# Preparing the S5 constants on GpSimd instead of VectorE, with the preparation's start moved, in a two-layer streaming encoder

## The chip, the cores and the metric

The kernel runs on one core of a Trainium2 chip. The metric is the device time of one execution in microseconds (us); the median of several runs counts. TensorE is called PE here, VectorE DVE, ScalarE ACT, GpSimd POOL and SyncE SP, as in the profile.

## The reference, cut to what matters

A trunk of two layers works on 256 positions of width 1024 in float32. Each layer is an FFN, a mixer and a second FFN, each added to the residual stream with a norm before and after.

```python
def reference(x, ...):
    for l in range(DEPTH):                      # DEPTH = 2
        f1 = swiglu(rmsnorm(x, g[0]), gate[l, 0], up[l, 0], down[l, 0])
        x = x + 0.5 * rmsnorm(f1, g[1])
        m = hybrid_mixer(rmsnorm(x, g[2]), ...)
        x = x + rmsnorm(m, g[3])
        f2 = swiglu(rmsnorm(x, g[4]), gate[l, 1], up[l, 1], down[l, 1])
        x = x + 0.5 * rmsnorm(f2, g[5])
```

The mixer projects the stream once, runs an S5 state-space model and a chunked attention with a relative bias on parts of it, and merges the two through gates. The S5 part needs constants that depend on its parameters alone:

```python
dt = exp(log_dt); mag = exp(lr * dt); ang = li * dt
ab_re, ab_im = mag * cos(ang), mag * sin(ang)
den = lr * lr + li * li
f_re = ((ab_re - 1) * lr + ab_im * li) / den
f_im = (ab_im * lr - (ab_re - 1) * li) / den
bb = f * b                                      # complex
```

The kernel also needs cos and sin of `ang` times 1, 2, 4, ... 64, to build tables of rotations by a position within a chunk. All of it is computed on the chip, once for each layer.

## The kernel before

**Weights.** All weight matrices are read from HBM in 368 chunks of 128 x 1024 float32, 184 for each layer: 66 for the first FFN, 52 for the mixer, 66 for the second FFN. A chunk lands in a `raw` buffer (`load`, line 461), ACT rounds it to a high part `wh` and DVE subtracts that from the chunk to get the low part `wl` (`halves`, line 467). Each product is then three matmuls: high by high, high by low, low by high. For every third chunk from 44 to 65 of a layer (`ADDED`) the subtraction is a DMA instead: ACT writes `-wh` into `wl` and POOL starts a DMA that adds the chunk to it (`add_to`, line 380). SP issues all loads.

**Positions.** The 256 positions are two tiles of 128, t=0 and t=1. Chunk i is used for both, t=1 some chunks behind t=0.

**Blocks of an FFN.** The hidden width is cut into six blocks. A block has eight chunks for gate and up, and four down chunks of the block before it are worked in. In some blocks (`SEVEN`: 1 and 3 in the first FFN, 1 to 4 in the second) gate and up for both tiles are formed by seven products in place of eight (`seven`, line 649). They need sums and differences of eight chunks, which lie in eight `raw` buffers for that time; some of these sums are made by DVE, those of `BY_DMA` by DMA adds that POOL starts.

**Buffers.** `SLOTS` gives 33 `blk` (128 x 512), 12 `raw`, 8 `wh`, 8 `wl`, 8 PSUM banks `ps`, and a few small ones. Buffers of the classes in `ORDERED` are handed out in the order of due times.

**The order.** Nothing is issued as it is written. Every operation is recorded with an engine, a planned cost, its inputs and outputs and a stream; `schedule` (line 209) then works back from the consumers to a due time for every operation (with a margin, `MARGIN`, where one stream feeds another) and simulates the engines, giving each the ready operation that is due first. The result is one fixed order for each engine, and every engine works through its own in order, waiting where an input or a buffer isn't ready.

**The preparation.** `prep(l)` (line 797) is recorded once for each layer before its mixer, in the stream `prep` with a margin of 40 us. Nothing of it may start before the first matmul of chunk `PREP_AT[l]` for t=0, and the loads of the attention's bias not before that of chunk `BIAS_AT` of the layer:

```python
after = [self.g.ops[self.mark[(0, PREP_AT[l])]]]
...
early = [self.g.ops[self.mark[(0, l * LAYER_CHUNKS + BIAS_AT)]]]
```

Once that gate is open, `constants` (line 781) takes `raw` buffers for `mt` and for the two rotation tables `E` and lets POOL set their first columns. The parameters come by DMA into `prm`. Then some 80 short operations on DVE, through the helpers `tt` (line 376), `stt` (395) and `ts` (400), form `dt` and `mag` by a polynomial exponential on 16 columns, the angles on 16 and then 112 columns (7 multiples of 16), their sine and cosine, and the factors `fr` and `fi`. ACT spreads `mag2` into `mt`. Wider operations follow on DVE: the complex products `cmul` and the doubling steps for `E`; ACT and PE put `BT`, `CT` and `D0` together. The mixer's S5 part (`s5`) reads all of these.

**POOL's queue.** Besides the memsets of the preparation POOL starts the DMA adds and computes the reciprocal square root of every norm as a power (`pow`, line 391), all in one queue.

Of the kernel before, what the change touches and what calls it, by code (L numbers as in the profile page):

```python
# [17 lines left out]
ALU = mybir.AluOpType  # L18
AX = mybir.AxisListType

P = 128
# [18 lines left out]
LAG = 3  # L40
TAU = 1.395
MARGIN = {"pre": 10.0, "edge": 4.0, "conv": 7.558, "conv0": 3.423, "task": 7.748, "att0": 37.576, "s50": 37.749, "att1": 28.585, "sums": 3.0, "s51": 29.753, "prep": 40.0}
PREP_AT = (3, 149)
BIAS_AT = 50
LOOK = 0.027
CAP = 5.417
WARM = 16
# [18 lines left out]
class View:  # L66
# [50 lines left out]
    def ap(self):  # L117
        t = self.buf.tile
        for s in self.steps:
            t = s(t)  # L120
        return t
# [202 lines left out]
class Kern:  # L324
# [51 lines left out]
    def tt(self, out, a, b, op):  # L376
        return self.g.op("dve", 0.07 + a.free_size() / 960, [out], [a, b],
                         lambda: self.nc.vector.tensor_tensor(out=out.ap(), in0=a.ap(), in1=b.ap(), op=op))  # L378
# [16 lines left out]
    def stt(self, out, a, s, b, op0=ALU.mult, op1=ALU.add):  # L395
        cost = 0.07 + a.free_size() / 960 + 0.061 * isinstance(s, View)
        return self.g.op("dve", cost, [out], [a, s, b], lambda: self.nc.vector.scalar_tensor_tensor(  # L397
            out=out.ap(), in0=a.ap(), scalar=ap(s), in1=b.ap(), op0=op0, op1=op1))

    def ts(self, out, a, s1, s2=None, op0=ALU.mult, op1=ALU.add):  # L400
        def fn():
            if s2 is None:
                self.nc.vector.tensor_scalar(out=out.ap(), in0=a.ap(), scalar1=ap(s1), scalar2=None, op0=op0)
            else:
                self.nc.vector.tensor_scalar(out=out.ap(), in0=a.ap(), scalar1=ap(s1), scalar2=s2, op0=op0, op1=op1)  # L405
        cost = 0.07 + a.free_size() / 1920 + 0.061 * isinstance(s1, View)
        return self.g.op("dve", cost, [out], [a, s1], fn)
# [389 lines left out]
    def prep(self, l):  # L797
        self.mode("prep", "bulk")
        if l == 0:
            self.S = [self.own(f"st{i}", [P, PAIRS, 65], F32) for i in range(2)]  # L800
        after = [self.g.ops[self.mark[(0, PREP_AT[l])]]]
        self.constants(after)
# [5 lines left out]
        self.bias = [[self.blk() for _ in range(2)] for _ in range(2)]  # L808
        early = [self.g.ops[self.mark[(0, l * LAYER_CHUNKS + BIAS_AT)]]]
        for par in range(2):  # L810
            for u in range(2):
                b = self.bias[par][u].rearrange("p (h k) -> p h k", k=256)
# [1 line left out]
                self.memset("pool", b[0:64, :, 192:256], MASK)  # L814
        self.prm = prm
        lr, li = prm[:, SP_LR:SP_LR + 16], prm[:, SP_LI:SP_LI + 16]
        ts, tt, stt = self.ts, self.tt, self.stt

        def tmp(nmx):
            return self.own(f"pt_{nmx}", [P, 16], F32)  # L820

        def exp(o, xin):
            n, r, p = tmp("en"), tmp("er"), tmp("ep")
            ib = self.own("pt_ei", [P, 16], I32)
            ts(n, xin, math.log2(math.e), MAGIC)
            ts(n, n, MAGIC, op0=ALU.subtract)
            stt(r, n, -0.693359375, xin)
            stt(r, n, 2.12194440054690583e-4, r)
            ts(p, r, 1.0 / 5040)
            for k in (720, 120, 24, 6, 2, 1):  # L830
                stt(p, p, 1.0 / k, r, ALU.add, ALU.mult)
            ts(n, n, -127.0, 128.0, ALU.max, ALU.min)
            ts(n, n, 127.0, 8388608.0, ALU.add, ALU.mult)
            self.copy(ib, n)
            stt(o, p, 1.0, ib.bitcast(F32), ALU.add, ALU.mult)

        dt, ld, mag, mag2 = tmp("dt"), tmp("ld"), tmp("mag"), tmp("mag2")
        exp(dt, prm[:, SP_DT:SP_DT + 16])
        tt(ld, lr, dt, ALU.mult)
        exp(mag, ld)  # L840
        tt(mag2, mag, mag, ALU.mult)
        self.mag2 = mag2
        self.act(self.mt[:, :, 1:], mag2.spread(63), AF.Copy)

        wk = [self.blk() for _ in range(2)]
        ang, k, z, sn, cs, m, a = (wk[i // 4][:, (i % 4) * 112:(i % 4) * 112 + 112] for i in range(7))
        angv = ang.rearrange("p (e j) -> p e j", j=16)
        tt(angv[:, 0, :], li, dt, ALU.mult)
        for e in range(1, 7):
            ts(angv[:, e, :], angv[:, 0, :], float(2 ** e))  # L850
        ts(k, ang, 2.0 / math.pi, MAGIC)
# [4 lines left out]
        stt(ang, k, -c1, ang)  # L856
        stt(ang, k, -c2, ang)
        stt(ang, k, -c3, ang)
        tt(z, ang, ang, ALU.mult)
        ts(sn, z, 1.0 / 362880)  # L860
        for q in (-1.0 / 5040, 1.0 / 120, -1.0 / 6):
            stt(sn, sn, q, z, ALU.add, ALU.mult)
# [8 lines left out]
        stt(a, m, -1.0, m, ALU.mult, ALU.max)  # L871
        ts(k, a, -1.0, 1.0)
        ts(a, a, -1.0, 2.0)
        tt(m, m, a, ALU.mult)
        ecs = self.own("ecs", [P, 7, 16], F32)
        esn = self.own("esn", [P, 7, 16], F32)
        ef, sf = ecs.rearrange("p e j -> p (e j)"), esn.rearrange("p e j -> p (e j)")
        tt(ef, cs, k, ALU.mult)
        tt(a, sn, m, ALU.mult)
        tt(ef, ef, a, ALU.subtract)  # L880
        tt(sf, sn, k, ALU.mult)
        tt(a, cs, m, ALU.mult)
        tt(sf, sf, a, ALU.add)
        self.ecs, self.esn = ecs, esn

        ar, ni, nr, den, fr, fi, q = (tmp(s) for s in ("ar", "ni", "nr", "den", "fr", "fi", "q"))
        tt(ar, mag, ecs[:, 0, :], ALU.mult)
        ts(nr, ar, 1.0, op0=ALU.subtract)
        tt(ni, mag, esn[:, 0, :], ALU.mult)
        tt(den, lr, lr, ALU.mult)  # L890
        tt(q, li, li, ALU.mult)
        tt(den, den, q, ALU.add)
        self.recip(den, den)
        tt(fr, nr, lr, ALU.mult)
        tt(q, ni, li, ALU.mult)
        tt(fr, fr, q, ALU.add)
        tt(fr, fr, den, ALU.mult)
        tt(fi, ni, lr, ALU.mult)
        tt(q, nr, li, ALU.mult)
        tt(fi, fi, q, ALU.subtract)  # L900
        tt(fi, fi, den, ALU.mult)

        def half(t, i):
            return t[:, 256 * i:256 * i + 256].rearrange("p (j h) -> p j h", h=16)
# [51 lines left out]
        for e in range(6):  # L956
            k = 2 ** e
# [369 lines left out]
```

## Time and profile before

| | us |
|---|---|
| median of 3 runs | 1128.24 |
| lowest and highest | 1126.39, 1130.42 |
| the profiled execution | 1127.01 |
| its span | 1125.2 |

The span runs from the first to the last instruction in the profile; the mean granted clock of PE in it is 0.997 of full speed. The profile gives each engine's busy time, and for each instruction its start, its length and what the engine waited for before it. Operations that go through a helper carry the helper's line, so the names of the buffers tell them apart. PE's matmuls are pipelined, and one of 128 x 512 is shown longer than the distance to the next.

### The profile page before, as it was taken

The page shows a single profiled execution, that of the slowest core. Times are in us where ns is not written, and L with a number is a line of the kernel's source. Part 1 is how long each engine was busy: PE and PEld are TensorE (multiplying, and loading weights), DVE is VectorE, ACT ScalarE, POOL GpSimd, SP SyncE. Part 2 cuts the span into 40 slices and gives each one's busy share as a digit, 9 for nine tenths or more (in the row PEclk, how much of TensorE's full clock was granted, in tenths as well). Part 3 has the DMA queues.
Part 4 walks back from the last instruction along what each step waited for, and adds up shares of the span by engine and source line. Part 5 has one row for each costly group of instructions (what it writes and reads, how often), then busy time and mean ns, then how long its engine had stood idle before and what let it go on. Part 6 is the DMA issues. An engine that isn't in the chain of part 4 may idle for free.

```text
span 1125.2 us, 15956 instructions
## 1 busy us (share of the span) xinstructions
PE 1107.9 (98%) x5728; PEld 885.6 (79%) x5728; DVE 954.2 (85%) x1402; ACT 749.1 (67%) x1066; POOL 99.4 (9%) x131
## 2 busy tenths in 40 slices
PE   8999999999999999999999999999999999999997
PEld 6778788777788888788887888887777888888886
DVE  6998995895977899899899689778959679999983
ACT  6957686647754697577577476856486546878752
POOL 1101111000000031010030011100000002111100
PEclk9999999999999999999999999999999999999999
DMA  9885997545275557899658669964535664789941
GB/s 343 228 314 129 328 295 235 169 136 164 97 251 197 179 122 217 269 283 278 243 162 263 229 181 325 276 213 148 170 112 181 195 212 143 214 219 268 293 167 38
DMA packets 69487, 238.61 MB, mean 212 GB/s; under 512 B 8096, under 2 KB 8864, under 8 KB 69408
## 3 DMA queue, kind: packets, MB, share of 16 engines
q1 hardware_dynamic: 60192, 204.03, 51.2%
q0 software_dynamic: 9216, 33.56, 16.3%
q8 instruction: 45, 0.74, 0.3%
q14 instruction: 34, 0.28, 0.1%
HBM read 202.96 MB, written 1.05 MB: 181 GB/s over the span
## 4 chain that ended last, share of the span: by engine, by line
PE 87%; DVE 5%; issue 2%; ACT 2%; DMA 2%; POOL 1%; SPq 0%; POOLq 0%; DVEq 0%; ACTq 0%
PE ps L418 81%; PE ps L432 4%; DVE wl L378 3%; DMA raw<-in_wall_dram 2%; PE ps L424 1%; DVE blk L378 1%; ACT blk L371 1%; POOL s L393 1%; ACT wh L371 1%; DVE blk L397 1%; DVE raw L378 0%; SPq L354 0%; DVE x L397 0%; DVE s L405 0%; POOLq L1322 0%
## 5 line engine op out<-in xcount | busy, mean ns | idle before, releaser
L418 PE MATMUL ps<-wh,blk 128*128 128x512 f32 x2848 | 878.0, 400 | 4.5 <-DVE blk L378 2.3
L418 PEld LDWEIGHTS ps<-wh,blk 128*128 128x128 f32 x2848 | 530.4, 188 | 127.6 <-DVE blk L378 3.9
L371 ACT ACTIVATE wh<-raw 128x1024 fp32r<-128x1024 f32 (+1 forms) x442 | 456.9, 1053 | 261.0 <-PE ps L418 200.4
L378 DVE TENSOR_TENSOR wl<-raw,wh 128x1024 fp32r<-128x1024 f32 (+1 forms) x426 | 505.7, 1215 | 104.3 <-ACT wh L371 103.7
L418 PE MATMUL ps<-wl,blk 128*128 128x512 f32 x1424 | 524.4, 399 | 0.9 <-DVE wl L378 0.8
L418 PEld LDWEIGHTS ps<-wl,blk 128*128 128x128 f32 x1424 | 267.5, 188 | 63.4 <-DVE wl L378 2.5
L371 ACT ACTIVATE blk<-ps 128x512 fp32r<-128x512 f32 (+4 forms) x156 | 86.5, 561 | 54.8 <-PE ps L432 30.2
L378 DVE TENSOR_TENSOR blk<-ps,blk 128x512 fp32r<-128x512 f32 (+2 forms) x164 | 109.4, 672 | 13.1 <-ACT blk L371 12.7
L432 PE MATMUL ps<-ident,blk 128*128 128x128 f32 x432 | 74.7, 273 | 0.0
L382 POOL DMA_DIRECT2D raw<-raw x48 | 41.6, 867 | 341.3 <-ACT raw L371 261.8
L393 POOL TENSOR_TENSOR s<-s,mhalf 128x1 f32<-128x1 f32 x24 | 32.1, 1338 | 448.3 <-DVE s L405 448.2
L371 ACT ACTIVATE blk<-blk 32x128 f32<-32x128 f32 (+4 forms) x148 | 59.1, 400 | 12.4 <-DVE blk L378 8.6
L432 PEld LDWEIGHTS ps<-ident,blk 128*128 128x128 f32 x432 | 54.6, 140 | 15.9 <-PE ps L418 1.3
L371 ACT ACTIVATE blk<-ps,s 128x512 f32<-128x512 f32 (+1 forms) x68 | 43.7, 655 | 24.6 <-PE ps L418 20.4
L378 DVE TENSOR_TENSOR raw<-raw,raw 128x1024 f32<-128x1024 f32 x48 | 58.1, 1219 | 0.1
L371 ACT ACTIVATE raw<-raw 128x1024 f32<-128x1024 f32 x48 | 50.2, 1053 | 4.3 <-DVE raw L378 3.9
L378 DVE TENSOR_TENSOR blk<-blk,blk 128x512 f32<-128x512 f32 (+3 forms) x70 | 42.3, 627 | 0.0
L371 ACT ACTIVATE blk<-blk,s 128x128 f32<-128x128 f32 (+2 forms) x76 | 34.6, 486 | 6.7 <-DVE blk L378 6.6
L397 DVE SCALAR_TENSOR_TENSOR blk<-blk,s,blk 128x512 f32<-128x512 f32 x44 | 32.0, 746 | 0.9 <-ACT blk L371 0.8
L397 DVE SCALAR_TENSOR_TENSOR blk<-ps,s,blk 128x512 f32<-128x512 f32 (+1 forms) x24 | 15.8, 658 | 9.7 <-ACT blk L371 9.4
L382 POOL DMA_DIRECT2D wl<-raw x16 | 13.8, 865 | 111.7 <-ACT wl L371 56.3
L378 DVE TENSOR_TENSOR blk<-ps,raw 128x512 f32<-128x512 f32 x32 | 19.8, 681 | 4.2 <-PE ps L418 4.2
(100 smaller groups left out, 434.0 us busy)
## 6 DMA issues: line engine op xcount, KB each, us to landing
raw<-in_wall_dram SPq DMA_DIRECT2D x366, 512.0 KB, 5.3
raw<-raw POOLq DMA_DIRECT2D x48, 512.0 KB, 5.3
wl<-raw POOLq DMA_DIRECT2D x16, 512.0 KB, 7.2
gain<-in_gains_dram SPq DMA_DIRECT2D x22, 256.0 KB, 4.3
blk<-in_bias_dram SPq DMA_DIRECT2D x8, 256.0 KB, 4.8
raw<-in_wall_dram SPq DMA_DIRECT2D x4, 256.0 KB, 4.3
blk<-in_sp_dram SPq DMA_DIRECT2D x4, 256.0 KB, 9.3
x<-in_x_dram SPq DMA_DIRECT2D x3, 256.0 KB, 5.8
```

Source lines behind the costliest of these rows:

```text
L371: self.nc.scalar.activation(out=out.ap(), in_=in_.ap(), func=func, **k)
L378: lambda: self.nc.vector.tensor_tensor(out=out.ap(), in0=a.ap(), in1=b.ap(), op=op))
L382: lambda: self.nc.gpsimd.dma_start(out=out.ap(), in_=in_.ap(), accum_op=ALU.add), func="dma")
L393: lambda: self.nc.gpsimd.tensor_tensor(out=out.ap(), in0=a.ap(), in1=b.ap(), op=ALU.pow))
L397: return self.g.op("dve", cost, [out], [a, s, b], lambda: self.nc.vector.scalar_tensor_tensor(out=out.ap(), in0=a.ap(), scalar=ap(s), in1= ...
L418: return self.g.op("pe", cost, [out], [lhsT, rhs], lambda: self.nc.tensor.matmul(out.ap(), lhsT=lhsT.ap(), rhs=rhs.ap(), start=start, stop ...
L424: self.nc.tensor.matmul(out.ap(), lhsT=lhsT.ap(), rhs=rhs.ap(), start=start, stop=stop)
L432: lambda o=o, s=s: self.nc.tensor.transpose(o.ap(), s.ap(), self.ident.ap()))
```

## The change

Three constants change, and within `prep` the arithmetic goes to POOL. The new local helpers `ptt`, `ts` and `stt` issue POOL instructions. A `stt` (two arithmetic steps with a constant between two tensors) becomes two POOL instructions with a buffer between them. Forms with a `max`, the cast to integers and the reciprocal stay on DVE. From `cmul` on `prep` uses `self.tt` of DVE as before, since `tt` keeps its meaning.

```diff
-PREP_AT = (3, 149)
-BIAS_AT = 50
+PREP_AT = (26, 206)
+BIAS_AT = 62
...
-        ts, tt, stt = self.ts, self.tt, self.stt
+        tt = self.tt
+        gp = self.nc.gpsimd
+
+        def put(out, ins, fn):
+            self.g.op("pool", 0.25 + out.free_size() * 0.0022, [out], ins, fn)
+
+        def ptt(out, a, b, op):
+            put(out, [a, b], lambda: gp.tensor_tensor(out=out.ap(), in0=a.ap(), in1=b.ap(), op=op))
+
+        def ts(out, a, s1, s2=None, op0=ALU.mult, op1=ALU.add):
+            if op0 == ALU.max:
+                self.ts(out, a, s1, s2, op0, op1)
+            elif s2 is None:
+                put(out, [a], lambda: gp.tensor_scalar(out=out.ap(), in0=a.ap(), scalar1=s1, scalar2=None, op0=op0))
+            else:
+                put(out, [a], lambda: gp.tensor_scalar(out=out.ap(), in0=a.ap(), scalar1=s1, scalar2=s2, op0=op0, op1=op1))
+
+        def stt(out, a, s, b, op0=ALU.mult, op1=ALU.add):
+            if op1 == ALU.max:
+                return self.stt(out, a, s, b, op0, op1)
+            n = out.free_size()
+            mid = self.own(f"pt_mid{n}", [P, n])
+            ts(mid, a, s, op0=op0)
+            ptt(out, mid, b, op1)
...
-        tt(ld, lr, dt, ALU.mult)
+        ptt(ld, lr, dt, ALU.mult)
         exp(mag, ld)
-        tt(mag2, mag, mag, ALU.mult)
+        ptt(mag2, mag, mag, ALU.mult)
...
-        tt(ef, cs, k, ALU.mult)
-        tt(a, sn, m, ALU.mult)
-        tt(ef, ef, a, ALU.subtract)
+        ptt(ef, cs, k, ALU.mult)
+        ptt(a, sn, m, ALU.mult)
+        ptt(ef, ef, a, ALU.subtract)
...
-        tt(fi, fi, q, ALU.subtract)
-        tt(fi, fi, den, ALU.mult)
+        ptt(fi, fi, q, ALU.subtract)
+        ptt(fi, fi, den, ALU.mult)
```

Every other `tt` between the exponentials and `cmul` becomes `ptt` in the same way.

## Rows read from the trace of the kernel before

**Rows 1.** The page: busy time of the engines, share of the span, instructions.
```profile
PE 1107.9 (98%) x5728; PEld 885.6 (79%) x5728; DVE 954.2 (85%) x1402; ACT 749.1 (67%) x1066; POOL 99.4 (9%) x131
```

**Rows 2.** Stretches: start:end length, PE, PEld, DVE, ACT, POOL busy (instructions), clock, DMA share, GB/s.
```profile
120.00:130.00 10.00, 9.52 (x41) 7.39 (x41) 9.97 (x29) 7.40 (x8) 1.74 (x2) 1.00 1.04 327
...
450.00:460.00 10.00, 10.00 (x44) 7.74 (x42) 6.44 (x7) 3.21 (x5) 0.00 (x0) 1.00 1.01 296
460.00:470.00 10.00, 7.21 (x23) 5.31 (x23) 9.62 (x14) 5.22 (x7) 0.00 (x0) 0.83 0.90 355
```

**Rows 3.** Timeline of ACT: start, length, what it did [idle before <-what ended it].
```profile
458.35 5.79 ACT L371 ACTIVATE wh<-raw 128x1024 fp32r<-128x1024 f32 x6 [6.79 <-DMA raw<-in_wall_dram]
...
1013.74 2.96 ACT L371 ACTIVATE wh<-raw 128x1024 fp32r<-128x1024 f32 x3 [2.91 <-PE ps L418]
```

**Rows 4.** Timeline of POOL in the second FFNs of both layers.
```profile
417.41 0.13 POOL L359 MEMSET raw<- 128x16 f32 x1 [0.45 <-DVE wl L378]
...
447.09 0.86 POOL L382 DMA_DIRECT2D raw<-raw  x1 [2.60 <-DVE raw L378]
...
512.50 0.86 POOL L382 DMA_DIRECT2D raw<-raw  x1 [2.90 <-DVE raw L378]
...
1002.73 0.86 POOL L382 DMA_DIRECT2D raw<-raw  x1 [2.54 <-DVE raw L378]
...
1063.90 0.86 POOL L382 DMA_DIRECT2D raw<-raw  x1 [3.09 <-DVE raw L378]
```

**Rows 5.** Timeline: gating products, a power, the bias loads; last, the matmuls reading `raw`.
```profile
85.19 0.74 DVE L397 SCALAR_TENSOR_TENSOR blk<-ps,s,blk 128x512 f32<-128x512 f32 x1
...
641.60 0.74 DVE L397 SCALAR_TENSOR_TENSOR blk<-ps,s,blk 128x512 f32<-128x512 f32 x1
...
194.04 0.56 POOL L393 TENSOR_TENSOR s<-s,mhalf 128x1 f32<-128x1 f32 x1 [0.19 <-DVE s L405]
...
187.12 1.81 SPq L354 DMA_DIRECT2D blk<-in_bias_dram  x4
...
L418 PE MATMUL ps<-blk,raw x128: 270/275/377, 218.8 to 845.7; 128*128 128x128 f32 x128
```

**Rows 6.** Groups by form: count, busy us, mean ns of one, idle time before.
```profile
L397 DVE SCALAR_TENSOR_TENSOR blk<-blk 128x112 f32<-128x112 f32 x16 | 4.3, 268 | 0.1
...
L403 DVE TENSOR_SCALAR blk<-blk 128x16 f32<-128x16 f32 x12 | 1.1, 168 | 0.1
...
L359 POOL MEMSET raw<- 128x16 f32 x6 | 0.6, 122 | 1.5 <-DVE wl L378 1.5
...
masks.py:199 POOL TENSOR_SCALAR_AFFINE_SELECT ident<-ident 128x128 f32<-128x128 f32 x1 | 0.3, 292 | 0.1
```

**Rows 7.** The power's line: least, median and longest ns, first and last start.
```profile
L393 POOL TENSOR_TENSOR s<-s,mhalf x24: 547/554/5472, 16.7 to 1119.8; 128x1 f32<-128x1 f32 x24
```

**Rows 8.** Timeline of POOL and DVE around a long power.
```profile
396.80 5.47 POOL L393 TENSOR_TENSOR s<-s,mhalf 128x1 f32<-128x1 f32 x1 [6.83 <-DVE s L405]
...
401.79 0.74 DVE L397 SCALAR_TENSOR_TENSOR blk<-ps,s,blk 128x512 f32<-128x512 f32 x1
```

**Rows 9.** Groups of DVE by form between 82 and 145 us.
```profile
L378 DVE TENSOR_TENSOR wl<-raw,wh 128x1024 fp32r<-128x1024 f32 x25 | 29.9, 1221 | 9.3 <-ACT wh L371 9.3
...
L378 DVE TENSOR_TENSOR blk<-ps,blk 128x512 f32<-128x512 f32 x5 | 3.4, 683 | 0.0
...
L378 DVE TENSOR_TENSOR blk<-ps,blk 128x512 fp32r<-128x512 f32 x3 | 2.0, 683 | 0.0
```

**Rows 10.** Timeline of POOL, DVE and ACT; last, DMA adds from 80 to 200 us, to landing.
```profile
105.61 0.87 POOL L382 DMA_DIRECT2D raw<-raw  x1 [10.74 <-ACT raw L371]
...
100.45 3.50 DVE L378 TENSOR_TENSOR wl<-raw,wh 128x1024 fp32r<-128x1024 f32 x3 [3.33 <-ACT wh L371]
...
110.21 4.65 DVE L378 TENSOR_TENSOR wl<-raw,wh 128x1024 fp32r<-128x1024 f32 x4
...
116.26 2.96 ACT L371 ACTIVATE wh<-raw 128x1024 fp32r<-128x1024 f32 x3 [2.67 <-PE ps L418]
...
raw<-raw POOLq DMA_DIRECT2D x4, 512.0 KB, 5.7
```

More of the change, by code (lines that the diff above doesn't have):

```diff
@@ L847, in prep @@
         angv = ang.rearrange("p (e j) -> p e j", j=16)
-        tt(angv[:, 0, :], li, dt, ALU.mult)
+        ptt(angv[:, 0, :], li, dt, ALU.mult)
         for e in range(1, 7):
@@ L858, in prep @@
         stt(ang, k, -c3, ang)
-        tt(z, ang, ang, ALU.mult)
+        ptt(z, ang, ang, ALU.mult)
         ts(sn, z, 1.0 / 362880)
@@ L873, in prep @@
         ts(a, a, -1.0, 2.0)
-        tt(m, m, a, ALU.mult)
+        ptt(m, m, a, ALU.mult)
         ecs = self.own("ecs", [P, 7, 16], F32)
@@ L877, in prep @@
         ef, sf = ecs.rearrange("p e j -> p (e j)"), esn.rearrange("p e j -> p (e j)")
-        tt(ef, cs, k, ALU.mult)
-        tt(a, sn, m, ALU.mult)
-        tt(ef, ef, a, ALU.subtract)
-        tt(sf, sn, k, ALU.mult)
-        tt(a, cs, m, ALU.mult)
-        tt(sf, sf, a, ALU.add)
+        ptt(ef, cs, k, ALU.mult)
+        ptt(a, sn, m, ALU.mult)
+        ptt(ef, ef, a, ALU.subtract)
+        ptt(sf, sn, k, ALU.mult)
+        ptt(a, cs, m, ALU.mult)
+        ptt(sf, sf, a, ALU.add)
         self.ecs, self.esn = ecs, esn
         ar, ni, nr, den, fr, fi, q = (tmp(s) for s in ("ar", "ni", "nr", "den", "fr", "fi", "q"))
-        tt(ar, mag, ecs[:, 0, :], ALU.mult)
+        ptt(ar, mag, ecs[:, 0, :], ALU.mult)
         ts(nr, ar, 1.0, op0=ALU.subtract)
[L889 to L892, printed above, removed]
+        ptt(ni, mag, esn[:, 0, :], ALU.mult)
+        ptt(den, lr, lr, ALU.mult)
+        ptt(q, li, li, ALU.mult)
+        ptt(den, den, q, ALU.add)
         self.recip(den, den)
[L894 to L899, printed above, removed]
-        tt(fi, fi, q, ALU.subtract)
-        tt(fi, fi, den, ALU.mult)
+        ptt(fr, nr, lr, ALU.mult)
+        ptt(q, ni, li, ALU.mult)
+        ptt(fr, fr, q, ALU.add)
+        ptt(fr, fr, den, ALU.mult)
+        ptt(fi, ni, lr, ALU.mult)
+        ptt(q, nr, li, ALU.mult)
+        ptt(fi, fi, q, ALU.subtract)
+        ptt(fi, fi, den, ALU.mult)
         def half(t, i):
```

## The prediction

> **What bounds the kernel now.** I read the page's busy times first: PE is busy for 1107.9 of 1125.2 us, DVE for 954.2, POOL for 99.4 [rows 1]. So 17.3 us of PE idle time is all that a better order can win, and work taken off DVE gains nothing unless PE was waiting for it. Next I cut the span into stretches of 10 us and looked for those in which PE is not full. Away from the start and the end the deepest is 460 to 470: PE is busy for 7.21 us, starts 23 matmuls where the stretch before it starts 44, and its granted clock falls to 0.83 [rows 2]; part of the stretch ran at the lower of its two levels, 1.2 GHz, after PE had idled. That is in the second FFN of layer 0. The second FFN of layer 1 has the same work and no such stretch.
>
> The timeline says why. At 458.35 ACT had stood 6.79 us because a weight load was late; at the same place in layer 1 ACT waited 2.91 us for PE instead: there the weights were ahead [rows 3]. A load needs one of 12 `raw` buffers. At 417.41 POOL sets the first columns of `mt` and, right after, of the two `E` tables for layer 1 [rows 4]; from then on these hold three of the twelve. `PREP_AT[1] = 149` lets them start there, where four blocks in a row use the seven-product form, each with eight `raw` of its own. What the stall costs is read from DMA adds that correspond in the two FFNs: before it they lie 1002.73 - 447.09 = 555.64 us apart, after it 1063.90 - 512.50 = 551.40 [rows 4]. That is **4.2 us**. The count agrees: 21 matmuls too few at 10/44 = 0.23 us are 4.8 us.
>
> **The change part by part.** *`PREP_AT`.* For layer 1 the gate moves from chunk 149 to 206, chunk 22 of the next FFN. The gating product behind chunk 27 for t=0 stands at 641.60 [rows 5]; 12 matmuls a chunk at 0.23 us are 2.7 us, so chunk 22 begins near 641.6 - 6 x 2.7 = 625. The three `raw` and the parameter load leave the second FFN of layer 0: **-4.2 us** (ends -4.8, and 0 if another load is late in its place). The FFN that they move into holds those buffers today as well, and has no such stall. For layer 0 the gate moves from chunk 3 to 26, near 85.19 - 2 x 2.7 = 80 us [rows 5], and more `raw` is free until then; PE hardly idles there, so I count nothing. S5 first reads the prepared tables at 218.8 us [rows 5]: 138 us remain.
>
> *`BIAS_AT`.* The gate moves from chunk 50 to 62 of 66. The first FFN's end is marked by the reciprocal root at 194.04, so chunk 62 begins near 194 - 4 x 2.7 = 183. The bias loads are issued at 187.12 today [rows 5], held by `blk` buffers and not by the gate: 0.
>
> *DVE work removed.* Per layer 49 operations on 16 columns and 29 on 112. Twelve of the narrow ones take 1.1 us together, 0.09 each, and a wide one 0.27 at most [rows 6]: 49 x 0.09 + 29 x 0.27 = 12 us a layer at most. PE covers nearly all of it: in the stretch where the wide ones of layer 0 stand, 120 to 130, PE idles 0.48 us [rows 2]. So at most **-0.5 us**, in layer 0 alone.
>
> *POOL work added.* A `stt` becomes two instructions, so 67 on 16 columns and 41 on 112 per layer, 108 in all. No row shows such an operation on POOL. From below: a memset of 16 columns, 122 ns, and an affine select of 128, 292 ns [rows 6]: 67 x 0.122 + 41 x 0.292 = 20 us a layer. From above: the one two-input operation there is, a power on one column, median 554 ns [rows 7]: 108 x 0.554 = 60 us. A power is a dearer function than a product, so I take 25 us, near the lower end.
>
> These are hidden only while POOL gets to run. A power started at 396.80 and took 5.47 us; it ended 0.48 us after 401.79, when DVE's unbroken run of operations with two SBUF inputs gave way to one that reads PSUM [rows 8]. Three more of the 24 went that way. So a POOL read waits until DVE idles or reads PSUM. Between 82 and 145 us DVE idles 9.3 us, spends 3.4 + 2.0 us in its two largest groups with a PSUM input [rows 9], and loses some 7 us of preparation: about 22 us free for 25 us of POOL work, with 73 us more until S5. It just about fits. The Trainium skill, "SBUF — State Buffer", section "Who interferes with whom", says that a DVE instruction with two SBUF inputs and a GpSimd instruction that reads SBUF contend, and that whichever issues first keeps the shared ports for its whole length; the first half agrees with the power of 5.47 us, and POOL holding up DVE in its turn is what no row here shows. By it DVE would lose up to the 25 us and save 12, and the sum would be worse than mine.
>
> *Handovers.* The two `max` forms, the cast and the reciprocal stay on DVE, so DVE waits for POOL at some six places a layer and ACT waits for `mag2`. Queued behind them are DVE's weight splits and PSUM evacuations and ACT's conversions, and PE waits for those. Cover: the weights are ahead by what ACT waits for PE, as 2.67 us before 116.26 [rows 10]. From 0, where a wait fits into that, to 3 us and more a layer, where it doesn't; I take 0.5 each, since each wait also stops DVE and so lets POOL run: **+1.0**.
>
> **Sum:** -4.2 - 0.5 + 1.0 = -3.7 us. The profiled execution took 1127.01 us, 1.8 more than its span; the median of the runs, 1128.24, is 1.2 above that. From the median: 1128.2 - 3.7 = **1124.5 us**.
>
> **The rivals.** *Given back in part.* POOL lags where DVE is dense, and a handover lasts longer than the weights are ahead: 1 to 3 us a layer more than I took, 1126.5 to 1130.5. For it: 22 us free for 25. Against it: each lag ends itself, as above.
>
> *The POOL queue becomes the bound: slower.* POOL issues the DMA adds too. At 105.61 and just after it starts the two that make the last product's weights of a seven-product block, and their conversion begins at 116.26, when a buffer comes free [rows 10]. DVE runs almost without a gap on two-input splits from 100.45 to 114.86 [rows 10]. If one preparation read is queued ahead of the adds and not done by 100.45, the adds go out at 114.9 and 115.8 and land 5.7 us later [rows 10], at 121.5, 5.2 us after 116.26 with PE right behind: 10.4 us in two layers, 1128.2 - 4.2 + 10.4 = **1134.4**. It decides from an add issued later than 116.3 - 5.7 = 110.6. For it: the power that stood 5.47 us. Against it: from 82 to 100 DVE has gaps enough for some 40 narrow operations, nearly both exponentials, and ACT waiting for `mag2` would break DVE's run.
>
> *The stall stays.* If the loads at 450 are late for another reason (the DMA share is 1.01 there [rows 2]), the move of the gate does nothing: 1128 to 1129. Against it: layer 1's FFN loads as much.
>
> **How the numbers follow.** A measurement of this kernel tells 0.3%, 3.4 us, from no change: faster is below 1124.9, slower above 1131.6. The forecast gets 0.41, given back in part 0.27, the stall staying 0.06, the POOL queue 0.26; so faster 0.41, same 0.33, slower 0.26. The range begins at 1121.5 (the stall at 4.8 us, the DVE relief, no handover cost, and a little over 1 us from the freed buffers) and reaches to 1134.0, up to the slower rival; its far part, with POOL at 0.55 us an operation, is left out. The forecast's own range is 1122 to 1126.5.
>
> **What would show it.** Right: the stretch near 460 is full at clock 1.00 and ACT there waits for PE; the adds that correspond in the two second FFNs keep one distance from first to last, where today it drops by 4.2 us; POOL is busy about 150 us; its operations are short where DVE idles and stretched over DVE's runs. Wrong: the adds of 91 to 107 come several us later against the matmuls, with PE waiting for `wl` behind them; or DVE waits over 3 us for POOL at a `max` or at the first complex product.

## The result and the profile after

The median after is **1144.9 us** (four runs, 1144.61 to 1145.41) beside 1127.32 for the kernel before on the same chip: a ratio of 1.0154, with an interval of 1.014 to 1.0167. The change makes the kernel slower by some 17.6 us; forecast were 1124.5 us and a range up to 1134.0. The profiled execution took 1144.65 us, its span 1142.9.

The page's busy times, to be held against [rows 1]:

```profile
PE 1113.4 (97%) x5728; PEld 888.9 (78%) x5728; DVE 938.1 (82%) x1246; ACT 750.2 (66%) x1066; POOL 206.5 (18%) x347
```

DVE lost 16.1 us of work, 8 a layer. POOL gained 107.1, or 53.6 a layer, in 216 instructions. That is 0.50 us each where the forecast took 0.23.

Where the time went is read by FFN. The powers on POOL mark the same places of the work in both kernels. Timeline of POOL, kernel before (for the first two places see 194.04 in [rows 5] and 396.80 in [rows 8]), the end of layer 0's second FFN and the start of layer 1's second FFN:

```profile
581.15 5.40 POOL L393 TENSOR_TENSOR s<-s,mhalf 128x1 f32<-128x1 f32 x1 [6.89 <-DVE s L405]
...
952.45 5.47 POOL L393 TENSOR_TENSOR s<-s,mhalf 128x1 f32<-128x1 f32 x1 [6.83 <-DVE s L405]
```

The same view of the kernel after, with all four places:

```profile
207.35 0.57 POOL L393 TENSOR_TENSOR s<-s,mhalf 128x1 f32<-128x1 f32 x1
...
410.13 5.47 POOL L393 TENSOR_TENSOR s<-s,mhalf 128x1 f32<-128x1 f32 x1 [6.83 <-DVE s L405]
...
589.51 5.40 POOL L393 TENSOR_TENSOR s<-s,mhalf 128x1 f32<-128x1 f32 x1 [6.79 <-DVE s L405]
...
969.92 5.47 POOL L393 TENSOR_TENSOR s<-s,mhalf 128x1 f32<-128x1 f32 x1 [6.83 <-DVE s L405]
```

After minus before is 13.3 us at the end of layer 0's first FFN, 13.3 after its mixer, 8.4 after its second FFN and 17.5 at the end of layer 1's mixer. So the second FFN of layer 0 won 5.0 us, and the two first FFNs, where the preparation now runs, lost 13.3 and 9.1. The mixers, which use the constants, lost nothing.

The stretches show both. Columns as in [rows 2]:

```profile
120.00:130.00 10.00, 5.03 (x20) 3.77 (x19) 2.69 (x3) 3.18 (x4) 9.28 (x21) 0.79 1.02 270
130.00:140.00 10.00, 8.71 (x33) 6.71 (x32) 7.23 (x9) 4.95 (x6) 9.41 (x18) 0.87 0.90 263
460.00:470.00 10.00, 10.00 (x45) 8.12 (x44) 10.00 (x10) 7.62 (x8) 1.72 (x2) 1.00 0.96 221
680.00:690.00 10.00, 6.55 (x29) 4.95 (x27) 4.05 (x5) 1.48 (x2) 8.86 (x16) 0.95 1.00 263
690.00:700.00 10.00, 7.37 (x26) 5.94 (x27) 6.73 (x9) 7.38 (x8) 9.57 (x16) 0.71 1.03 370
```

460 to 470 is full, at a clock of 1.00. At 120 the picture is unlike that of a busy machine: PE, DVE and ACT are all idle for half of the time or more, and POOL alone is full. They wait for it or for each other, as the timeline shows. PE pays twice, since its granted clock falls to 0.79 and 0.71 in such stretches: after it idles, part of them runs at 1.2 GHz.

Timeline around it, lines of POOL, DVE, ACT and PE (start, length, what, idle before):

```profile
88.21 0.22 POOL L824 TENSOR_TENSOR pt_er<-pt_mid,pt_er 128x16 f32<-128x16 f32 x1
...
104.45 0.17 DVE L405 TENSOR_SCALAR pt_en<-pt_en 128x16 f32<-128x16 f32 x1 [5.62 <-POOL pt_mid L830]
...
110.65 8.47 DVE L378 TENSOR_TENSOR wl<-raw,wh 128x1024 fp32r<-128x1024 f32 x7
110.93 1.29 POOL L830 TENSOR_SCALAR pt_mid<-blk 128x112 f32<-128x112 f32 x1
112.30 0.86 POOL L824 TENSOR_TENSOR pt_ep<-pt_mid,pt_er 128x16 f32<-128x16 f32 x1
113.13 1.40 POOL L824 TENSOR_TENSOR blk<-pt_mid,blk 128x112 f32<-128x112 f32 x1
114.50 1.23 POOL L830 TENSOR_SCALAR pt_mid<-pt_ep 128x16 f32<-128x16 f32 x1
...
119.81 0.93 POOL L382 DMA_DIRECT2D raw<-raw  x1
...
123.20 0.49 POOL L830 TENSOR_SCALAR pt_mid<-blk 128x112 f32<-128x112 f32 x1
...
125.42 1.06 ACT L371 ACTIVATE wh<-raw 128x1024 fp32r<-128x1024 f32 x1 [6.18 <-DMA raw<-raw]
...
128.49 0.76 PE L418 MATMUL ps<-wh,blk 128*128 128x512 f32 x1 [4.97 <-DVE blk L378]
...
132.47 0.27 DVE L397 SCALAR_TENSOR_TENSOR blk<-blk 128x112 f32<-128x112 f32 x1 [4.13 <-POOL blk L824]
```

Two things are to be seen. First the lengths: the same product of 16 columns takes 0.22 us at 88.21, while DVE leaves gaps, and 0.86 at 112.30, under DVE's run of seven splits from 110.65 to 119.12. The wide ones take 0.49 at 123.20 and 1.29 to 1.41 under the run. The seven splits take 8.47 / 7 = 1.21 us each, and in that run POOL starts about one operation for each of them: a read gets in behind one DVE operation, not behind the whole run. Second the queue: the add that stood at 105.61 before [rows 10] stands behind these reads in POOL's order and goes out at 119.81. ACT waits 6.18 us for it, DVE's next run waits for ACT, and PE waits 4.97.

The wait of 4.13 us at 132.47 is another one: there DVE waits for POOL at the `max` in the sine, one of the handovers. Layer 1 repeats both, and the conversion behind the late add and the `max` stand within two microseconds of one another. Timeline, same columns:

```profile
686.44 1.06 ACT L371 ACTIVATE wh<-raw 128x1024 fp32r<-128x1024 f32 x1 [7.11 <-DMA raw<-raw]
...
688.16 0.28 DVE L397 SCALAR_TENSOR_TENSOR blk<-blk 128x112 f32<-128x112 f32 x1 [5.95 <-POOL blk L824]
...
692.63 0.76 PE L418 MATMUL ps<-wh,blk 128*128 128x512 f32 x1 [6.09 <-ACT wh L371]
```

Groups by form over the whole span, POOL's four largest of the preparation (count, busy us, mean ns, idle before):

```profile
L830 POOL TENSOR_SCALAR pt_mid<-blk 128x112 f32<-128x112 f32 x24 | 19.5, 814 | 1.5
L824 POOL TENSOR_TENSOR blk<-pt_mid,blk 128x112 f32<-128x112 f32 x24 | 17.6, 733 | 0.8
L830 POOL TENSOR_SCALAR pt_mid<-pt_ep 128x16 f32<-128x16 f32 x28 | 15.7, 559 | 2.1
...
L824 POOL TENSOR_TENSOR pt_ep<-pt_mid,pt_er 128x16 f32<-128x16 f32 x24 | 12.5, 521 | 1.6
```

A line of the plan helps here. The diff gives the planner 0.25 + 0.0022 n us for an operation on n columns: 0.285 and 0.496 us, and for 67 and 41 of them 39.5 us a layer. POOL took 53.6. By these sums the order of every engine was laid out for a POOL that needs 14 us less in each layer than the real one, and engines that work through a fixed order cannot step round a late neighbour.

### The profile page after: what moved, and what is told of

Same layout as the page of the kernel before. It is cut to its first block, busy times and chain, and to the rows that moved or that the text cites. A ratio compares the mean times of both kernels' runs of the same rounds, so it can differ in the third digit from the quotient of the medians.

```text
span 1142.9 us, 16020 instructions
## 1 busy us (share of the span) xinstructions
PE 1113.4 (97%) x5728; PEld 888.9 (78%) x5728; DVE 938.1 (82%) x1246; ACT 750.2 (66%) x1066; POOL 206.5 (18%) x347
## 3 DMA queue, kind: packets, MB, share of 16 engines
q0 software_dynamic: 9216, 33.56, 16.1%
## 4 chain that ended last, share of the span: by engine, by line
PE 79%; POOL 8%; ACT 3%; DMA 3%; issue 3%; DVE 3%; SPq 0%; POOLq 0%; DVEq 0%; ACTq 0%
PE ps L418 74%; PE ps L432 4%; POOL pt_mid L830 3%; POOL blk L824 2%; DMA wl<-raw 2%; ACT blk L371 2%; PE ps L424 1%; ACT wh L371 1%; DVE wl L378 1%; POOL blk L830 1%; DVE blk L378 1%; POOL pt_ep L824 1%; DMA blk<-in_bias_dram 1%; DMA x<-in_x_dram 0%; DVE blk L397 0%
## 5 line engine op out<-in xcount | busy, mean ns | idle before, releaser
L371 ACT ACTIVATE blk<-blk 32x128 f32<-32x128 f32 (+4 forms) x148 | 59.1, 400 | 18.4 <-DVE blk L378 11.1
L378 DVE TENSOR_TENSOR blk<-blk,blk 128x512 f32<-128x512 f32 (+1 forms) x68 | 42.1, 641 | 0.0
L397 DVE SCALAR_TENSOR_TENSOR blk<-blk,s,blk 128x512 f32<-128x512 f32 x44 | 32.3, 755 | 2.3 <-ACT blk L371 1.6
L397 DVE SCALAR_TENSOR_TENSOR blk<-ps,s,blk 128x512 f32<-128x512 f32 (+1 forms) x24 | 15.8, 660 | 15.3 <-ACT blk L371 13.6
L359 POOL MEMSET blk<- 128x512 f32 (+1 forms) x26 | 12.6, 550 | 76.3 <-DMA blk<-in_bias_dram 42.6
```

Of the source, the lines that this page charges most:

```text
L359: lambda: getattr(self.nc, name).memset(out.ap(), v), after=after)
L371: self.nc.scalar.activation(out=out.ap(), in_=in_.ap(), func=func, **k)
```

## The experiments

**The theories.** *A, reads held up:* POOL's reads of SBUF wait for DVE's operations with two SBUF inputs, so POOL runs behind a plan that knows nothing of it, and all that was ordered after it comes late. *B, the queue alone:* the loss is in the DMA adds behind POOL's operations. *C, the handovers:* the loss is in DVE's waits for POOL at the clamps and the cast of the exponentials, at the `max` in the sine and at the first operations on the finished tables. *D, the gates:* the new places of the preparation cost it, on whatever engine it runs. Ratios are to the kernel before, in the same session, with their 95% intervals; diffs are against the kernel after unless said otherwise.

**1. The gates by themselves (D).** Against the kernel before:

```diff
-PREP_AT = (3, 149)
-BIAS_AT = 50
+PREP_AT = (26, 206)
+BIAS_AT = 62
```

> Only the three constants change; the preparation stays on DVE. Theory Q (the loss comes from POOL: its preparation reads each wait for a DVE operation, and DMA adds, DVE and ACT wait behind them): the stall near 460 us goes and nothing else comes, 1122 to 1123 us, 5 us below before. Rival G (the preparation that starts later is late for S5, wherever it runs): 1130 us or more. Rival R (the plan's new order costs by itself): between.

1123.28 us, 0.9964 [0.995, 0.9977]. By the powers after the mixers and after layer 0's second FFN, layer 0's first FFN gets 2.2 us longer, its second 4.8 shorter, and the rest stays. The stretch that was 7.21 us busy in [rows 2]:

```profile
460.00:470.00 10.00, 10.00 (x44) 8.04 (x44) 10.00 (x12) 7.73 (x9) 0.00 (x0) 1.00 1.03 413
```

So the stall was the gate's, D falls, and the move to POOL by itself costs 1144.9 - 1123.3 = 21.6 us. A second kernel moves the gate of layer 1 alone:

```diff
-PREP_AT = (3, 149)
+PREP_AT = (3, 206)
```

> The kernel before with one number changed: the gate of layer 1 at chunk 206 in place of 149; layer 0 keeps chunk 3, the preparation stays on DVE. With both gates moved (the run with the gates alone) the first FFN of layer 0 ended 2.2 us later than before, the second 4.8 us sooner against that. If the 2.2 us come from layer 0's later gate, this gives 1121 to 1122 us, the fastest so far; if they are an accident of the new plan, 1122 to 1124.

1121.92 us, 0.9955 [0.994, 0.997]: the fastest kernel here that forms the constants, ahead of both. Its interval overlaps that of the three constants together, so whether the later gate of layer 0 costs something is not settled by the times. Nor is it by the powers. After layer 0's mixer it has 2.7 us less than before and the other 2.2 more, but its 2.7 are there before any of the preparation: the second power of the span starts at 22.32 in place of 25.19, because the first took 0.85 us here and 3.73 in the kernel before.

**2. POOL's work without reads (A).** Each operation of the preparation on POOL is replaced by two memsets of its output, at the same planned cost; the kernel leaves the arithmetic out:

```diff
         def put(out, ins, fn):
-            self.g.op("pool", 0.25 + out.free_size() * 0.0022, [out], ins, fn)
+            def two():
+                gp.memset(out.ap(), 0.25)
+                gp.memset(out.ap(), 0.25)
+
+            self.g.op("pool", 0.25 + out.free_size() * 0.0022, [out], ins, two)
```

> The changed kernel with each of the 108 POOL operations a layer replaced by two memsets of its output (the arithmetic of the S5 constants is left out); plan, order and handovers are the same, but POOL reads nothing. Theory Q with waits of reads for DVE's two-input operations: POOL's operations end in 0.1 to 0.4 us also over DVE's runs, the adds come at their time, 1122 to 1126. If the length of the queue or the planned order is to blame and not the reads: 1138 to 1146.

1121.82 us, 0.9949 [0.9933, 0.9965]. The loss is gone. The order, the waits of DVE and ACT for POOL and the places in POOL's queue are those of the kernel after; POOL issues more instructions, 563 in all. Timeline of its POOL and a stretch of its windows:

```profile
102.60 0.19 POOL L823 MEMSET pt_mid<- 128x112 f32 x1
102.74 0.10 POOL L822 MEMSET pt_ep<- 128x16 f32 x1
...
106.75 0.87 POOL L382 DMA_DIRECT2D raw<-raw  x1 [3.15 <-ACT raw L371]
```

```profile
120.00:130.00 10.00, 10.00 (x45) 8.11 (x44) 8.51 (x14) 6.22 (x7) 7.01 (x48) 1.00 1.04 326
```

The add goes out 1.1 us after its place in [rows 10], and 120 to 130 is full. Two memsets of 112 columns are 0.38 us where a free read takes 0.42 to 0.49, so this kernel also has less to do. But free operations of 0.24 and 0.43 us would come to 34 us a layer, still under the planned 39.5: what breaks the plan is what reads take over and above that.

**3. The plan told of it (A).** POOL's work and the gates stay; the planner's price goes up to 0.54 and 0.78 us (68 us a layer), or half way (54 us, about what POOL takes):

```diff
-            self.g.op("pool", 0.25 + out.free_size() * 0.0022, [out], ins, fn)
+            self.g.op("pool", 0.5 + out.free_size() * 0.0025, [out], ins, fn)
```

> The changed kernel, but the planner prices a POOL operation at 0.5 + 0.0025 per column in place of 0.25 + 0.0022, about what they took. Theory Q: the planned order puts the adds and the handovers where POOL really is, so most of the 23 us lost in the two first FFNs comes back, 1126 to 1134. Rival L (POOL and DVE hold each other up at the shared ports, so that DVE is short of time whatever the order): 1142 to 1147.

1129.24 us, 1.0019 [1.0009, 1.003], inside the range that theory A gave. A stretch of its windows:

```profile
120.00:130.00 10.00, 10.00 (x45) 8.10 (x44) 7.43 (x9) 7.56 (x8) 9.46 (x17) 1.00 1.03 338
```

POOL is as busy as in the kernel after (203.4 us in all against 206.5), and as full in this stretch, yet PE is full too: the adds stand at 105.15 and 106.94. So it is not POOL's time by itself that costs, but that it runs behind the order. Of the 21.6 us 6.0 are left.

```diff
-            self.g.op("pool", 0.25 + out.free_size() * 0.0022, [out], ins, fn)
+            self.g.op("pool", 0.375 + out.free_size() * 0.00235, [out], ins, fn)
```

> The changed kernel with the planner's price half way to the run that priced POOL at 0.5 + 0.0025 (0.375 + 0.00235 per column). If the loss follows how far the plan is ahead of POOL, it lies between: 1131 to 1141. If it is an accident of one order, anywhere from 1122 to 1150.

1133.96 us, 1.0069 [1.005, 1.0088]: 10.7 us above the gates alone. With 39, 54 and 68 us planned for a layer, the loss is 21.6, 10.7 and 6.0. So a price that matches POOL's mean time takes back half; what makes up the rest was not followed further.

**4. The adds alone (B).** No DMA adds in the two first FFNs, ACT and DVE make those sums; once with the preparation on POOL, once (with the gates moved) on DVE:

```diff
-BY_DMA = ((3, 4), (3, 4))
+BY_DMA = ((), (3, 4))
...
-            self.ws[i] = self.halves(self.load(i, parts), parts, i % LAYER_CHUNKS in ADDED)
+            self.ws[i] = self.halves(self.load(i, parts), parts, i % LAYER_CHUNKS in ADDED and i % LAYER_CHUNKS >= FFN_CHUNKS)
```

> The changed kernel, but in the first FFN of each layer no sum and no low part is made by a DMA add: ACT and DVE make them, so POOL's queue holds only the preparation there. To be read against the same kernel with the preparation on DVE (next run). If the adds queued behind the reads are the whole loss, the two differ by at most 4 us; if DVE and ACT waiting at the handovers are, by 12 us and more.

> The control: gates moved, preparation on DVE, no DMA adds in the first FFNs. DVE gets 24 more operations of 1.2 us on two inputs: 1124 to 1135 us.

1167.14 us, 1.0357 [1.034, 1.0373], against 1130.99, 1.0037 [1.0023, 1.005]. The loss by POOL does not shrink, it grows to 36.2 us. B as the whole cause falls. The waits between 82 and 150 us of the first of the two (total, times, longest):

```profile
ACT raw L371 <- POOL pt_mag L824: 17.5, 1, 17.5
...
DVE blk L397 <- POOL blk L824: 10.7, 1, 10.7
PE ps L418 <- DVE blk L378: 10.6, 2, 9.9
```

With no add to be late, DVE is late, at the `max` in the sine (L397), and PE behind it. ACT stands longer still, for `mag2`, but PE's wait of 9.9 us ends at 140.78, behind DVE's, while ACT still waits.

**5. The handovers alone (C).** Clamps and cast go to POOL as well, so the exponentials need no DVE:

```diff
-            if op0 == ALU.max:
-                self.ts(out, a, s1, s2, op0, op1)
-            elif s2 is None:
+            if s2 is None:
...
-            self.copy(ib, n)
+            put(ib, [n], lambda: gp.tensor_copy(ib.ap(), n.ap()))
```

> The changed kernel with the clamp and the cast of both exponentials on POOL as well, so that DVE waits for POOL only from the sine's max on. If the handovers inside the exponentials make DVE and with it the weights late (5.6 us at the second clamp of layer 0), 4 to 6 us come back a layer: 1133 to 1138. If the adds behind the reads in POOL's own queue are the loss, it stays within 3 us of 1145.

1150.51 us, 1.0207 [1.0194, 1.0221], 5.6 slower than the kernel after and outside both of the ranges expected; so the clamps and the cast are not the cause. The `max` in the sine stays on DVE and still waits 4.8 us in layer 0, and the first operation on the tables 5.4. The waits between 82 and 150 us:

```profile
ACT wh L371 <- DMA raw<-raw: 11.7, 2, 9.7
PEld ps L418 <- issue: 10.2, 2, 8.1
PE ps L418 <- DVE blk L378: 9.4, 2, 7.7
```

Its first add of the pair stands at 121.38. PE's longest wait, 7.7 us, ends at 129.19, before the `max` at 133.82; it comes from the add, so C as the whole cause falls too. Take the adds away, and PE waits behind a handover; take the first handovers away, and it waits behind the adds. Both are ends of one lag.

**6. Shorter DVE operations (A).** Each weight split as two operations of 512 columns, with the preparation on POOL, and on DVE with the gates moved:

```diff
-            self.tt(wl[:, s], raw[:, s], wh[:, s].bitcast(F32), ALU.subtract)
+            w = min(512, s.stop - s.start)
+            for o in range(s.start, s.stop, w):
+                q = slice(o, o + w)
+                self.tt(wl[:, q], raw[:, q], wh[:, q].bitcast(F32), ALU.subtract)
```

> The changed kernel with each 1024-column weight split of DVE made as two of 512 columns. To be read against the next run, which does the same with the preparation on DVE. Theory: a POOL read waits for the one DVE operation in progress, so with DVE operations half as long it waits half as long; POOL operations over DVE's runs take 0.6 to 0.8 us in place of 1.2 to 1.4, and the loss against the control falls from 21.6 us to 12 or less. If a read waits for the end of a whole run of DVE, the loss stays at 20 us or more.

> The control: gates moved, preparation on DVE, weight splits in halves. DVE loses about 0.06 us on each of 422 splits, 25 us of work spread over the span: 1124 to 1132 us.

1142.32 us, 1.0145 [1.0126, 1.0163], and 1139.09, 1.0114 [1.0098, 1.013], the control above the 1132 expected at most. POOL now costs 3.2 us in place of 21.6. POOL's largest two groups with halved splits, and two stretches of that kernel:

```profile
L833 POOL TENSOR_SCALAR pt_mid<-blk 128x112 f32<-128x112 f32 x24 | 16.4, 684 | 1.7
L827 POOL TENSOR_TENSOR blk<-pt_mid,blk 128x112 f32<-128x112 f32 x24 | 14.6, 606 | 0.9
```

```profile
120.00:130.00 10.00, 5.53 (x23) 3.87 (x21) 3.55 (x7) 6.48 (x7) 9.05 (x23) 0.99 0.97 311
130.00:140.00 10.00, 7.44 (x24) 5.97 (x25) 7.36 (x13) 2.79 (x3) 10.00 (x22) 0.67 0.98 277
```

The reads got shorter, 684 and 606 ns for 814 and 733, and POOL's total fell by 12.5 us to 194.0. That a read's wait follows the length of a DVE operation is A's. That the loss goes with it is not shown. In layer 0 PE still idles 7.0 us in these two stretches, where it idled 6.3 in the kernel after and not at all in the control; the control loses 3.5 us later, between 160 and 180, where the kernel with POOL loses none. Only in layer 1 did the stall shrink, from 6.2 us between 670 and 710 to 2.4. By itself halving cost the control 15.8 us; with the preparation on POOL it won 2.6 against the kernel after.

**7. The old gates with POOL.** Gates 3 and 149 and 50 as before, preparation on POOL:

```diff
-PREP_AT = (26, 206)
-BIAS_AT = 62
+PREP_AT = (3, 149)
+BIAS_AT = 50
```

> The preparation on POOL at the planner's old price, but with the gates where they were (chunks 3 and 149). Layer 0's reads then fall into 20 to 70 us and layer 1's into the second FFN of layer 0, where DVE is busy over 95% and DMA adds follow each other all the way. If the loss is POOL's reads waiting for DVE, it is larger there: 1145 to 1165 us. If it needs the late gate (too little time to S5), it goes: 1127 to 1132.

1159.0 us, 1.0284 [1.0269, 1.0298], with POOL busy for 236.8 us, so the loss does not need the late gates. The moved gates are worth 14.1 us with the preparation on POOL, and 3.7 with it on DVE (1126.97 before, in that session, less 1123.28).

**8. How long a read waits.** The best of both, the high price and the gates 3 and 206:

```diff
-PREP_AT = (26, 206)
+PREP_AT = (3, 206)
...
-            self.g.op("pool", 0.25 + out.free_size() * 0.0022, [out], ins, fn)
+            self.g.op("pool", 0.5 + out.free_size() * 0.0025, [out], ins, fn)
```

> The preparation on POOL at the price of 0.5 + 0.0025 per column, with layer 0's gate back at chunk 3 and layer 1's at 206. If the plan's price is what matters, layer 0 has 50 us more for the same work and the kernel comes to 1121 to 1126. If reads where DVE is busiest cost by themselves (20 to 70 us), 1130 to 1140.

1136.9 us, 1.0094 [1.0073, 1.0115], 15.0 above the same gates with the preparation on DVE. By the power after layer 0's mixer, its first FFN is 13.3 longer than before. Timeline of POOL and ACT:

```profile
41.62 0.92 POOL L382 DMA_DIRECT2D raw<-raw  x1
42.29 13.77 POOL L824 TENSOR_TENSOR pt_er<-pt_mid,prm 128x16 f32<-128x16 f32 x1
...
56.02 0.21 POOL L824 TENSOR_TENSOR pt_q<-prm 128x16 f32<-128x16 f32 x1
...
56.81 0.91 POOL L382 DMA_DIRECT2D raw<-raw  x1
...
61.49 2.00 ACT L371 ACTIVATE wh<-raw 128x1024 fp32r<-128x1024 f32 x2 [10.43 <-DMA raw<-raw]
```

This one read of 16 columns stood for 13.77 us, through an unbroken run of DVE operations with two SBUF inputs from 41.54 to 55.98. The powers of 5.47 us are of that kind, and the kernel with the old gates has a read of 12.14 us. Timeline of its POOL:

```profile
41.66 0.26 POOL L830 TENSOR_SCALAR pt_mid<-pt_en 128x16 f32<-128x16 f32 x1
41.89 12.14 POOL L824 TENSOR_TENSOR pt_q<-prm 128x16 f32<-128x16 f32 x1
```

In the kernel after, none of the preparation's reads took over 2 us. The powers and the read of 13.77 began after POOL had idled or had started a DMA. Two kernels tried whether a pause between two reads brings the long wait on, with a memset behind each operation, of 256 columns and of 16; the read of 12.14, right behind another read, already speaks against it:

```diff
+        pad = self.own("pt_pad", [P, 256])
+
         def put(out, ins, fn):
-            self.g.op("pool", 0.25 + out.free_size() * 0.0022, [out], ins, fn)
+            def padded():
+                fn()
+                gp.memset(pad.ap(), 0.0)
+
+            self.g.op("pool", 0.25 + out.free_size() * 0.0022, [out, pad], ins, padded)
```

> The changed kernel; after each of its 108 POOL operations a layer POOL also sets a spare tile of 256 columns (some 0.3 us, no read). If a read that is queued right behind another read gets in after one DVE operation, and one that comes while DVE runs waits for the end of the run, then over DVE's runs POOL operations of 4 to 14 us appear, few and long, and the time goes to 1160 us or more. If every read waits for one DVE operation, none is longer than 2 us and only POOL's 32 us a layer of extra work is added: 1150 to 1160.

> The same with a spare tile of 16 columns, some 0.1 us. If a pause of any length between two reads lets DVE close the gap, as in the run before: operations of 4 to 14 us, 1155 us or more. If the next read is still early enough, POOL operations stay under 2 us and the time within 5 us of 1145.

1168.84 us, 1.0359 [1.0336, 1.0381], with POOL busy for 262.4 us, and 1140.57, 1.0112 [1.0094, 1.0129], with 226.4. No read of the preparation took over 2 us in either. So the first came out as slow as was expected with long waits, without having them, and the second is 4.3 us faster than the kernel after with 20 us more on POOL; neither was followed up. Timeline of the first, under a run of three splits from 108.19:

```profile
108.40 1.09 POOL L830 TENSOR_TENSOR pt_er<-pt_mid,pt_er 128x16 f32<-128x16 f32 x1
109.44 0.31 POOL L825 MEMSET pt_pad<- 128x256 f32 x1
109.83 0.86 POOL L836 TENSOR_SCALAR pt_ep<-pt_er 128x16 f32<-128x16 f32 x1
```

A pause of a few tenths of a microsecond does not bring on the long wait. What does is open.

## Why the prediction was wrong, point by point

**The stall: right.** Forecast -4.2, measured -5.0 in the change and -4.8 with the gates alone. The sign that was named held: the adds that correspond in the two second FFNs keep their distance, 1020.20 - 460.41 = 559.79 us early and 1081.36 - 521.49 = 559.87 late, where it dropped by 4.2 before.

**Layer 0's gate and the bias: nearly right.** Both were counted as nothing. In the one trace of the three constants layer 0's first FFN is 2.2 us longer; which of them did it, and whether it is beyond noise, the times don't settle.

**DVE relief: small, as said.** DVE was busy 8 us less a layer, of 12 at most. The memset kernel, where that work is gone and POOL harms nothing, is 1.5 us under the gates alone, with intervals that overlap; -0.5 cannot be told from it.

**POOL's work: the step that failed.** The forecast took 25 us a layer, near the lower end of 20 to 60, because a power is a dearer function than a product. 53.6 came out, near the upper end, the power's median of 0.554 us [rows 7]. Free of DVE, the lower end was the nearer one indeed, 0.20 to 0.29 us for 16 columns and 0.41 to 0.50 for most of 112, an estimate of some 34 us a layer. The rest, some 20 us, is the wait for DVE, which the same part of the prediction had found, and then used only to ask whether POOL's time fits into DVE's gaps. It was not added to the price of each operation.

**"It just about fits" and the handovers at 0.5 us a layer: wrong by the size that mattered.** The lag behind the order cost 13.3 and 9.1 us, or 11.1 and 9.0 against the gates alone, where 0.5 each was taken. Both signs named for being wrong came: the adds were late, with PE waiting behind them, and DVE waited 5.62 us at a `max`. Two readings went wrong. POOL does get in between DVE's operations, so the gaps were not the limit; and 73 us until S5 are no cover, because it is not S5 that waits. The adds, the clamps and the `max` in the sine have places in a fixed order, laid out with 39.5 us. The diff states the price from which that follows, and the forecast never held POOL's likely time against it.

**The ports.** The Trainium skill, "SBUF — State Buffer", section "Who interferes with whom", gives the shared ports to whichever of the two issued first. By it DVE was to lose up to 25 us. The trace disagrees for DVE: between 82 and 145 us its splits take 1263 ns in the mean, against 1221 before [rows 9], and 22 x 0.042 us is under 1 us.

**The rivals.** "The POOL queue becomes the bound" is what happened, at its place: the add went out at 119.81, past the stated 110.6, and its conversion ran at 125.42 in place of 116.26. It priced 10.4 us for two layers; the two first FFNs lost 22.4, and it stood at 0.26, behind the forecast. It put the lag down to one read that waits for a whole run, where it was dozens that wait for one operation each, and it took the adds for the only place, where experiments 4 and 5 show a second. The arguments against it, gaps enough and a DVE that stops itself, priced the operations at their free time.

## What to carry over

Before work is moved to an engine in a kernel with a planned order, compare the price that the plan is given with what an operation takes beside its neighbours there; if the plan is ahead of the engine, everything ordered after it is late, however much time there is until the result is used. A price near the measured time took back 10.9 of 21.6 us here, one a quarter above it 15.6, and leaving the work where it was took back all. When removing one waiting place only moves the wait, look for the lag that feeds both.

## What was not expected of the hardware

A short POOL read has mostly one of three lengths in these runs: 0.2 to 0.5 us with DVE idle or elsewhere, about one DVE operation (0.86 to 1.51 us in the kernel after, beside splits of 1.21) in a run of DVE operations with two SBUF inputs, and now and then the whole run (5.47, 12.14 and 13.77 us). A few lie between, up to 2.63. The memsets of experiment 2, which read nothing, run through at 0.10 to 0.22 us beside the same work (0.44 to 0.53 right behind the start of a DMA). DVE itself is hardly slowed: 1263 ns a split in place of 1221. What decides between one operation and a whole run is open.
